# A hybrid attention and convolution block: the first two value blocks in one group, three of six pair sums brought by transfer, and another deal of the layer-norm steps

## The chip, the cores and the metric

The kernel runs on one core of a Trainium2 chip. A core has a matrix engine (PE in the profile; PEld is its weight load), a vector engine (DVE), an activation engine (ACT), GpSimd (POOL) and a queue engine (SP) that issues most transfers. Each engine executes its own list of instructions strictly in order and waits on semaphores for the others. The metric is the device time of one execution, in microseconds (us).

## What is computed

One layer on a sequence of 256 positions with 4096 channels. After an RMS norm, one large product gives seven column groups, and two branches use them. Cut to what matters here:

```python
xn = rms_norm(x, norm_in_g)
q, k, v, z_a, a_c, g_c, z_c = split(xn @ w_in)      # each 2048 columns wide
y_a = rms_norm(chunked_attention(q, k, v, table)) * silu(z_a)      # 16 heads of 128
u   = a_c * sigmoid(g_c)                            # GLU
u   = silu(layer_norm(causal_depthwise_conv(u, 31 taps)))
y_c = rms_norm(u @ w_pw + b_pw) * silu(z_c)
h   = x + concat(y_a, y_c) @ w_out
h  += sigmoid(rms_norm(h) @ w_ple_gate + b) * (p @ w_ple)
out = rms_norm(h)
```

All is in float32. For the matrix engine each float32 operand is split into a high and a low part, and a product is three matmuls: high by high, low by high, high by low.

## The kernel before

**Tiles.** The 256 positions are two halves `h` of 128. A block is 512 output columns (`NB`). The 4096 input channels are 32 blocks of 128, or 16 pairs. One matmul multiplies 128 channels of one half with 512 columns.

**A single block** (`product`, line 235) takes 32 channel blocks x 2 halves x 3 = 192 matmuls. ACT makes the high part of each weight tile and DVE the low part (`parts_of`, lines 199 to 210: `wh` and `wl`, three buffers each).

**Two blocks as one group** (`mixed_product`, line 339) run over the 16 channel pairs. A plain pair costs 2 x 2 x 2 x 3 = 24 matmuls. A pair marked `*` or `+` is done by a Strassen-Winograd step: seven products in place of eight, 21 matmuls, at the price of sums of weight tiles. With `*` the DVE makes four sums for a pair (lines 464, 465, 471, 472: two into `ua`, two into `ub`). With `+` the first two sums come by transfer: SP loads one part into `ua` and GpSimd adds the other with an accumulating transfer (lines 417 and 418), and the DVE makes only the other two, in place. The orders in which the pairs are taken are the strings in lines 329 to 337; `early` has four `+` steps, `early_six` six `*` steps. From the first to the last such step the group holds all four temporary PSUM banks for its helper sums (`P1`, `P5`, `P7`, `P6`); the same four banks serve transposes and attention at other times. At the end ACT and DVE combine the helpers (`helper_sums`, line 505) and fold the accumulators into the result (line 533).

**Work dealt out in between.** Convolution taps and layer-norm steps are small DVE and ACT jobs in a queue (`later`). After each pair of a group, `fill(n)` takes n jobs from it (line 182); the numbers per pair are `early_fills`, `six_fills`, or `(4,)`.

**Order of the stages.** `glu_conv(c)` makes one input group (the columns `a_c` and `g_c` of block c as one pair), the GLU, and puts 124 taps in the queue. `heads(g)` makes q and k of four heads as one group, transposes them (`to_heads`), makes v as a single block and runs `attention`. The list before is: input groups 0 and 1, heads 0, input group 2, heads 1, input group 3, heads 2, the layer norm's jobs into the queue, heads 3. Then follow the pointwise product, the z groups, `w_out` and the gate. I call the groups glu0 to glu3, qk0 to qk3, v0 to v3, and the attention of four heads attn0 to attn3.

The text gives a program order. A planner in the framework moves instructions between each other's waiting times by its own estimates, so the order on each engine is written into the program when it is built, and does not adapt when it runs.

Of the kernel before, what the change touches and what calls it, by code (L numbers as in the profile page):

```python
# [25 lines left out]
def hybrid_block(  # L26
# [137 lines left out]
    def transposed(src, blocks, then=lambda ins: None):  # L164

        pt = tmp_psum()
        for i, b in enumerate(blocks):
            for h in range(NH):
                last_transpose[:] = [
                    nc.tensor.transpose(  # L170
                        pt[:, i * T + h * P : i * T + (h + 1) * P],
                        src[:, h, b * P : (b + 1) * P],
                        ident,
                    )
                ]
                then(*last_transpose)
        return [pt[:, i * T : (i + 1) * T] for i in range(len(blocks))]
# [151 lines left out]
    dense = units("1 0* 3 2* 5 4* 6* 7 8* 9 10* 11 12* 14* 13 15")  # L329
    first = units("0 1 3 5 7 9 11 13 15 2* 8 4* 10 6* 12 14")  # L330
    early = units("1 3 5 0+ 7 9 2+ 11 13 4+ 15 8 6+ 10 12 14")
    early_six = units("1 3 5 7 0* 9 2* 11 4* 13 6* 15 8* 10* 12 14")

    early_fills = (5, 6, 1, 5, 6, 1, 5, 6, 1, 5, 6, 1, 2, 5, 5, 4)
    six_fills = (4, 6, 7, 1, 5, 1, 5, 1, 5, 1, 2, 4, 6, 6, 6, 4)
    final = units("1 0* 3 2* 5 4* 6* 7 8* 9 10* 12* 11 13 14 15")
    late = units("1 3 5 7 9 11 13 15 0* 2 4* 6 8* 10* 12 14")

    def mixed_product(
# [86 lines left out]
        for n, (pair, seven) in enumerate(order):  # L426
            if n < done:
                continue
            if ahead:
                ahead(pair)  # L430
            wts = []
            for k in range(2):
                wt = wpool.tile([P, 2, NB], F32, tag="w", name="wt")
                if seven == "+" and k == 0:
                    nc.sync.dma_start(wt[:, 0], w[2 * pair * P : (2 * pair + 1) * P, col : col + NB])
                else:
                    nc.sync.dma_start(wt, two_columns(w, 2 * pair + k, col, apart))
                wts.append(wt)
            sums_ahead(n)
            if n >= len(order) - n_left:  # L440
                for k in range(2):
                    tiles = left[2 * (n - len(order) + n_left) + k]
                    held.append((2 * pair + k, parts_of(wts[k], 2, tiles and tiles())[0]))
                fill(fills[n % len(fills)])
                continue
            if not seven:
                for k in range(2):
                    add_plain(n, k, *parts_of(wts[k], 2)[0])
                fill(fills[n % len(fills)])
                continue  # L450
            begins = not helper
            if begins:
                for name in ("P1", "P5", "P7", "P6"):
                    helper[name] = ps_tmp.tile([P, NB], F32, tag="tmp", name=f"acc_{name}")
                banks.update(helper)
            w0, w1 = wts
            plus = partial(nc.vector.tensor_tensor, op=ALU.add)
            before = list(recent)
            w0h, w0l = parts_of(w0, 1)[0]
            if seven == "+":  # L460
                ua = ub = sums[n]
            else:
                ua = upool.tile([P, 2, NB], F32, tag="u", name="ua")
                plus(ua[:, 0], w0[:, 0], w0[:, 1])  # L464
                plus(ua[:, 1], w0[:, 1], w1[:, 1])  # L465
            with queued_behind(before if seven == "+" else ()):
                uah, ual = pair_parts(ua)
            w1h, w1l = parts_of(w1, 2)[0]
            if seven != "+":
                ub = upool.tile([P, 2, NB], F32, tag="u", name="ub")  # L470
            plus(ub[:, 0], ua[:, 0], w1[:, 1])
            plus(ub[:, 1], ub[:, 0], w1[:, 0])  # L472
# [12 lines left out]
            add("P3", s_of(3), (w1h[:, 1], w1l[:, 1]), n, True)  # L485
            add("P6", s_of(2), (ubh[:, 0], ubl[:, 0]), n, True)
            add("P4", block(k1, 1), (ubh[:, 1], ubl[:, 1]), n, True)
            if begins and on_begin:
                on_begin()
            if begins:  # L490
                tc.add_manual_dep(
                    made[first].ins, last_transpose[0].ins.name,
                    mybir.DependencyInfo(mybir.DependencyClass.NoSync, mybir.DependencyReason.DATA),
                    reason="transposes before the helpers take their banks",
                )
            if n == last_seven:
                on_helpers(helper)
            fill(fills[n % len(fills)])
# [12 lines left out]
        tt(z[1][0], helper["P7"], z[1][0], ALU.add)  # L511
        tt(z[1][1], helper["P5"], z[1][0], ALU.add)

    def sum_tiles():

        t = [spool.tile([P, NH, NB], F32, tag="stage", name="z") for _ in range(2)]
        return t, [[t[j][:, h] for j in range(2)] for h in range(NH)]

    def scaled_pair(w, col, apart, order, r, fills, **kw):

        t, z = [], []

        def on_helpers(helper):
            for dst, src in zip((t, z), sum_tiles()):
# [13 lines left out]

    def square_sum(dst, src, scale=1.0):
        junk = spool.tile([P, NB], mybir.dt.bfloat16, tag="junk", name="junk", bufs=1)  # L540
        return nc.scalar.activation(junk[:, : src.shape[1]], src, AF.Square, scale=scale, accum_out=dst)

    def rstd_of(partial, n, name):
        r = cpool.tile([P, partial.shape[1]], F32, name=name)
# [222 lines left out]
    def layer_norm_swish():  # L767
# [1 line left out]
        add = nc.vector.tensor_tensor  # L769
        st = {}  # L770

        def hd_tile(name):
            return spool.tile([P, 4, T], F32, tag="hd", name=name, bufs=5)
# [90 lines left out]
    y_a = []  # L864
    ssq_a = cpool.tile([P, NH, AW // NB], F32, name="ssq_a")

    def to_heads(st, name):

        t = spool.tile([P, GH, T], F32, tag="hd", name=name, bufs=5)
        for pair in range(GH // 2):  # L870
            pt = tmp_psum()
            for i in range(2):
# [9 lines left out]
            )  # L882
        return t

    def attention(g, qT, kT, v, bias):
        y = act.tile([P, NH, NB], F32, tag="act", name="y_a")
        for hd in range(GH):
            sp = tmp_psum()
            nc.tensor.matmul(sp[:, :P], qT[:, hd, :P], kT[:, hd, :P], start=True, stop=True)
# [25 lines left out]
            nc.tensor.matmul(o[:, HD : 2 * HD], pT[:, 2 * P :], v[:, 1, vc], start=False, stop=True)  # L915
            for h in range(NH):
                nc.scalar.activation(
                    y[:, h, vc], o[:, h * HD : (h + 1) * HD], AF.Identity, scale=den[:, h : h + 1]
                )
        for h in range(NH):  # L920
            square_sum(ssq_a[:, h, g : g + 1], y[:, h, :])
        y_a.append(y)

    def heads(g):
        nonlocal more
        bias = spool.tile([P, GH, T], F32, tag="hd", name="bias", bufs=5)
        span = 2 * MAXR + 1
        nc.sync.dma_start(
            bias,
# [9 lines left out]
        if g == n_g - 1:  # L939
            first_sums.close()  # L940
            more = pool("more", 4)
        accv = product(w_in0, o_v + g * NB, xT, KD)
        v = spool.tile([P, NH, NB], F32, tag="hd", name="v", bufs=5)
        for h in range(NH):
            nc.scalar.activation(v[:, h, :], accv[h], AF.Identity, scale=r_x[:, h : h + 1])
        attention(g, qT, kT, v, bias)

    n_g = H // GH
    assert n_g == CW // NB
# [68 lines left out]
    def gated(ys, c0, col, r_y, order, ahead):  # L1018
# [6 lines left out]

        acc = mixed_product(w_in0, col + c0 * NB, xT, xS, order, on_helpers, ahead=ahead, fills=(2,))
        for h, j in QUARTERS:
            zz, y = z[h][j], ys[c0 + j][:, h, :]
            tt(zz, acc[h][j], zz, ALU.subtract if j else ALU.add)  # L1029
            nc.scalar.activation(zz, zz, AF.Silu, scale=r_x[:, h : h + 1])  # L1030
            later.append(partial(stt, y, y, r_y[:, h : h + 1], zz, ALU.mult, ALU.mult))

    def before_last(make):
# [278 lines left out]
```

## Time and profile before

| | |
|---|---|
| median of 3 runs | 2039.11 us (2038.57 to 2039.72) |
| the profiled execution | 2040.98 us |
| its span, first to last instruction | 2039.2 us |
| PE busy | 2019.7 us, 99% |
| DVE busy | 1860.4 us, 91% |
| ACT busy | 1198.3 us, 59% |
| granted PE clock, mean | 0.997 |

The profile's views used here are these. The page gives busy time per engine. The table by stretches gives, for each stretch of time, the stretch's length and then the busy time and the number of instructions (x) of each engine, the granted clock, the share of the DMA engines that was busy and GB/s. The groups give for one line, operation and tile the count, the busy time, the mean duration in ns of one, and the idle time of the engine ahead of them with what ended it. The chain is the path of work that ended last, followed back from the end: start, length, what. The timeline gives single instructions in order of time, with the idle time before them in square brackets.

By the chain and the tiles' names the stages of the profiled execution lie so: glu0 to 102 us, glu1 to 187, qk0 to 270, v0 to 315, attn0 and glu2 to 408, qk1 to 495, v1 to 539, attn1 and glu3 to 633, qk2 to 716, v2 to 760, attn2 and qk3 to 860, v3 to 904.

### The profile page before, as it was taken

The page shows a single profiled execution, that of the slowest core. Times are in us where ns is not written, and L with a number is a line of the kernel's source. Part 1 is how long each engine was busy: PE and PEld are TensorE (multiplying, and loading weights), DVE is VectorE, ACT ScalarE, POOL GpSimd, SP SyncE. Part 2 cuts the span into 40 slices and gives each one's busy share as a digit, 9 for nine tenths or more (in the row PEclk, how much of TensorE's full clock was granted, in tenths as well). Part 3 has the DMA queues.
Part 4 walks back from the last instruction along what each step waited for, and adds up shares of the span by engine and source line. Part 5 has one row for each costly group of instructions (what it writes and reads, how often), then busy time and mean ns, then how long its engine had stood idle before and what let it go on. Part 6 is the DMA issues. An engine that isn't in the chain of part 4 may idle for free.

```text
span 2039.2 us, 26104 instructions
## 1 busy us (share of the span) xinstructions
PE 2019.7 (99%) x9106; PEld 1662.4 (82%) x9106; DVE 1860.4 (91%) x2640; ACT 1198.3 (59%) x1559; POOL 37.5 (2%) x43
## 2 busy tenths in 40 slices
PE   9999999999999999999999999999999999999997
PEld 7888888888888888788888888888888888888876
DVE  7999998699889977868899999999999999999998
ACT  7655446454555545666556566676565666655555
POOL 0000000000000000000000000000000000000000
PEclk9999999999999999999999999999999999999999
DMA  8787866876568866565666666676666656666765
GB/s 292 222 238 234 256 199 180 253 227 187 175 189 265 254 188 204 160 186 203 195 211 201 196 211 200 220 236 204 213 201 205 214 185 207 200 220 204 234 209 177
DMA packets 171839, 431.18 MB, mean 211 GB/s; under 512 B 13742, under 2 KB 16958, under 8 KB 171706
## 3 DMA queue, kind: packets, MB, share of 16 engines
q1 hardware_dynamic: 164528, 416.09, 63.2%
q0 software_dynamic: 6528, 12.58, 3.8%
q8 instruction: 71, 1.16, 0.2%
q10 hardware_dynamic: 650, 0.84, 0.1%
q14 instruction: 62, 0.51, 0.1%
HBM read 425.26 MB, written 4.19 MB: 211 GB/s over the span
## 4 chain that ended last, share of the span: by engine, by line
PE 91%; DVE 6%; issue 2%; DMA 0%; ACT 0%; POOLq 0%; POOL 0%; ACTq 0%; DVEq 0%
PE acc L382 65%; PE acc_P L382 16%; PE acc L229 7%; DVE wl L205 2%; DVE cv L718 2%; PE tmp_ps L170 1%; DMA wt<-in_w_in_dram 0%; PE tmp_ps L890 0%; PE tmp_ps L908 0%; PE tmp_ps L875 0%; PE tmp_ps L913 0%; PE acc L370 0%; PE tmp_ps L125 0%; DVE ul L205 0%; PE tmp_ps L915 0%
## 5 line engine op out<-in xcount | busy, mean ns | idle before, releaser
L382 PE MATMUL acc<-wh,big_t 128*128 128x512 f32 x3788 | 1172.0, 392 | 1.8 <-DVE z L1029 1.1
L204 ACT CAST wh<-wt 128x1024 fp32r<-128x1024 f32 (+1 forms) x737 | 715.7, 980 | 579.0 <-PE acc L382 353.6
L205 DVE TENSOR_TENSOR wl<-wt,wh 128x1024 fp32r<-128x1024 f32 (+1 forms) x737 | 824.5, 1131 | 91.3 <-ACT wh L204 86.0
L382 PEld LDWEIGHTS acc<-wh,big_t 128*128 128x128 f32 x3788 | 708.9, 188 | 149.1 <-ACT wh L204 1.5
L382 PE MATMUL acc<-wl,big_t 128*128 128x512 f32 x1894 | 732.3, 392 | 2.8 <-DVE wl L205 2.8
L382 PEld LDWEIGHTS acc<-wl,big_t 128*128 128x128 f32 x1894 | 355.8, 188 | 77.7 <-DVE wl L205 4.2
L718 DVE SCALAR_TENSOR_TENSOR cv<-uT,dw,cv 128x250 f32<-128x250 f32 (+21 forms) x480 | 200.5, 462 | 1.2
L204 ACT CAST uh<-ua 128x1024 fp32r<-128x1024 f32 x146 | 153.6, 1052 | 67.1 <-DVE ua L465 46.4
L205 DVE TENSOR_TENSOR ul<-ua,uh 128x1024 fp32r<-128x1024 f32 x146 | 177.9, 1218 | 7.6 <-ACT uh L204 7.4
L229 PE MATMUL acc<-wh,big_t 128*128 128x512 f32 x560 | 173.6, 390 | 0.0
L204 ACT CAST uh<-ub 128x1024 fp32r<-128x1024 f32 x98 | 103.1, 1052 | 98.5 <-DVE ub L472 70.6
L382 PE MATMUL acc_P<-uh,big_t 128*128 128x512 f32 x504 | 154.2, 391 | 0.1
L205 DVE TENSOR_TENSOR ul<-ub,uh 128x1024 fp32r<-128x1024 f32 x98 | 119.6, 1221 | 6.7 <-ACT uh L204 6.1
L229 PEld LDWEIGHTS acc<-wh,big_t 128*128 128x128 f32 x560 | 105.1, 188 | 21.6
L382 PEld LDWEIGHTS acc_P<-uh,big_t 128*128 128x128 f32 x504 | 93.5, 188 | 21.9 <-ACT uh L204 3.1
L229 PE MATMUL acc<-wl,big_t 128*128 128x512 f32 x280 | 108.9, 389 | 0.0
L382 PE MATMUL acc_P<-ul,big_t 128*128 128x512 f32 x252 | 96.5, 391 | 0.0
L464 DVE TENSOR_TENSOR ua<-wt 128x512 f32<-128x512 f32 x98 | 67.3, 687 | 22.6 <-DMA wt<-in_w_in_dram 17.0
L382 PE MATMUL acc<-uh,big_t 128*128 128x512 f32 x244 | 75.6, 390 | 0.0
L382 PE MATMUL acc_P<-wh,big_t 128*128 128x512 f32 x244 | 75.3, 389 | 0.0
L465 DVE TENSOR_TENSOR ua<-wt 128x512 f32<-128x512 f32 x98 | 67.1, 685 | 3.2 <-DMA wt<-in_w_in_dram 2.1
L472 DVE TENSOR_TENSOR ub<-ub,wt 128x512 f32<-128x512 f32 x98 | 67.3, 687 | 1.0
(244 smaller groups left out, 1575.6 us busy)
## 6 DMA issues: line engine op xcount, KB each, us to landing
wt<-in_w_in_dram SPq DMA_DIRECT2D x423, 512.0 KB, 4.4
wt<-in_w_out_dram SPq DMA_DIRECT2D x128, 512.0 KB, 4.3
wt<-in_w_ple_gate_dram SPq DMA_DIRECT2D x128, 512.0 KB, 4.1
wt<-in_w_pw_dram SPq DMA_DIRECT2D x32, 512.0 KB, 4.5
ua<-in_w_in_dram SPq DMA_DIRECT2D x24, 512.0 KB, 4.3
ua<-in_w_in_dram POOLq DMA_DIRECT2D x24, 512.0 KB, 8.2
wt<-in_w_in_dram SPq DMA_DIRECT2D x24, 256.0 KB, 2.7
hc<-in_x_dram SPq DMA_DIRECT2D x8, 512.0 KB, 5.3
```

Source lines behind the costliest of these rows:

```text
L170: nc.tensor.transpose(pt[:, i * T + h * P : i * T + (h + 1) * P], src[:, h, b * P : (b + 1) * P], ident,)
L204: nc.scalar.copy(wh[:, :kc, :], wt[:, :kc, :]),
L205: nc.vector.tensor_tensor(wl[:, :kc, :], wt[:, :kc, :], wh[:, :kc, :].bitcast(F32), ALU.subtract),
L229: nc.tensor.matmul(acc, a, b[:, k, :], start=kb == 0 and kind == 0, stop=kb == kblocks - 1 and kind == 2,)
L382: nc.tensor.matmul(banks[name], a, b, start=name not in begun, stop=final and ends[name] == n and kind == 2 and not (left and name in "P2 ...
L464: plus(ua[:, 0], w0[:, 0], w0[:, 1])
L465: plus(ua[:, 1], w0[:, 1], w1[:, 1])
L472: plus(ub[:, 1], ub[:, 0], w1[:, 0])
L718: nc.vector.scalar_tensor_tensor(cv[:, i, PAD - k :], uT[:, i, : T + k - PAD], dw[:, b, k : k + 1], cv[:, i, PAD - k :], ALU.mult, ALU.add,)
```

## The change

Three things are changed together, with some moving of buffers that makes room for them.

1. v0 and v1 are made as one group of two blocks (`paired_values(0, early, early_fills, ...)`) after qk0, with four `+` steps, and v1's single product is gone. Attention of heads 1 then follows directly on qk1. The heads' q tile moves to the pool `act`, and attention writes its result in place over it, seen through another view; the two value tiles take buffers of the pool `hd`.
2. The order of glu3, `early_six`, has three of its six steps as `+` in place of `*`, starts them at the fourth pair instead of the fifth, and its `*` steps make their second sums in place (one buffer fewer). `six_fills` is dealt anew.
3. qk3 gets `norm_fills` in place of `(4,)`: two jobs after three of the four `+` steps, five after most plain pairs; the sum stays 64.

```diff
-    early_six = units("1 3 5 7 0* 9 2* 11 4* 13 6* 15 8* 10* 12 14")
+    early_six = units("1 3 5 0+ 7 2* 9 4+ 11 6* 13 8+ 15 10* 12 14")
 
     early_fills = (5, 6, 1, 5, 6, 1, 5, 6, 1, 5, 6, 1, 2, 5, 5, 4)
-    six_fills = (4, 6, 7, 1, 5, 1, 5, 1, 5, 1, 2, 4, 6, 6, 6, 4)
+    six_fills = (6, 6, 1, 5, 1, 5, 1, 5, 1, 5, 1, 5, 1, 6, 7, 7)
+    norm_fills = (5, 5, 2, 5, 5, 2, 5, 5, 2, 5, 5, 2, 2, 4, 5, 5)
...
-                ua = upool.tile([P, 2, NB], F32, tag="u", name="ua")
+                ua = ub = upool.tile([P, 2, NB], F32, tag="u", name="ua")
                 plus(ua[:, 0], w0[:, 0], w0[:, 1])
                 plus(ua[:, 1], w0[:, 1], w1[:, 1])
...
-            if seven != "+":
+            if seven == "*" and not sums:
                 ub = upool.tile([P, 2, NB], F32, tag="u", name="ub")
...
-    def scaled_pair(w, col, apart, order, r, fills, **kw):
+    def scaled_pair(w, col, apart, order, r, fills, home={}, **kw):
...
-    def attention(g, qT, kT, v, bias):
-        y = act.tile([P, NH, NB], F32, tag="act", name="y_a")
+    def attention(g):
+        qT, kT, v, bias = qs[g], ks.pop(g), vs.pop(g), biases.pop(g)
+        y = qT.rearrange("q g (h d) -> q h g d", h=NH)
...
-        q, k = scaled_pair(w_in0, o_q + g * NB, o_k - o_q, early, r_x, (4,) if g == n_g - 1 else early_fills)
-        qT, kT = to_heads(q, "qT"), to_heads(k, "kT")
...
+    def keys(g, fills):
+        q, k = scaled_pair(w_in0, o_q + g * NB, o_k - o_q, early, r_x, fills)
+        qs[g] = act.tile([P, GH, T], F32, tag="act", name="qT")
+        to_heads(q, qs[g])
+        ks[g] = hd_tile("kT")
+        to_heads(k, ks[g])
+
+    def paired_values(g, order, fills, **kw):
+        vs[g], vs[g + 1] = scaled_pair(w_in0, o_v + g * NB, NB, order, r_x, fills, **kw)
...
     glu_conv(0)
-    for g in range(n_g):
-        if g + 1 < n_g:
-            glu_conv(g + 1)
-        else:
-            layer_norm_swish()
-        heads(g)
+    glu_conv(1)
+    load_bias(0)
+    keys(0, early_fills)
+    paired_values(0, early, early_fills, home=dict(tag="hd", bufs=5))
+    attention(0)
+    glu_conv(2)
+    load_bias(1)
+    keys(1, early_fills)
+    attention(1)
+    glu_conv(3)
+    load_bias(2)
+    keys(2, early_fills)
+    single_values(2)
+    attention(2)
+    layer_norm_swish()
+    load_bias(3)
+    keys(3, norm_fills)
+    first_sums.close()
+    more = pool("more", 4)
+    single_values(3)
+    attention(3)
```

The places that later read the attention's result (`square_sum`, `gated`, `transposed`) take the other view of the tile; their instruction counts stay.

More of the change, by code (lines that the diff above doesn't have):

```diff
@@ L171, in transposed @@
                         pt[:, i * T + h * P : i * T + (h + 1) * P],
-                        src[:, h, b * P : (b + 1) * P],
+                        src[:, h, b] if len(src.shape) == 4 else src[:, h, b * P : (b + 1) * P],
                         ident,
@@ L512, in helper_sums, with sum_tiles @@
         tt(z[1][1], helper["P5"], z[1][0], ALU.add)
-    def sum_tiles():
-        t = [spool.tile([P, NH, NB], F32, tag="stage", name="z") for _ in range(2)]
+    def sum_tiles(**kw):
+        kw = kw or dict(tag="stage")
+        t = [spool.tile([P, NH, NB], F32, name="z", **kw) for _ in range(2)]
         return t, [[t[j][:, h] for j in range(2)] for h in range(NH)]
-    def scaled_pair(w, col, apart, order, r, fills, **kw):
+    def scaled_pair(w, col, apart, order, r, fills, home={}, **kw):
         t, z = [], []
         def on_helpers(helper):
-            for dst, src in zip((t, z), sum_tiles()):
+            for dst, src in zip((t, z), sum_tiles(**home)):
                 dst.extend(src)
@@ L540, in square_sum @@
         junk = spool.tile([P, NB], mybir.dt.bfloat16, tag="junk", name="junk", bufs=1)
-        return nc.scalar.activation(junk[:, : src.shape[1]], src, AF.Square, scale=scale, accum_out=dst)
+        to = junk.rearrange("q (g d) -> q g d", d=src.shape[2]) if len(src.shape) == 3 else junk[:, : src.shape[1]]
+        return nc.scalar.activation(to, src, AF.Square, scale=scale, accum_out=dst)
     def rstd_of(partial, n, name):
@@ L770, in layer_norm_swish @@
         st = {}
-        def hd_tile(name):
-            return spool.tile([P, 4, T], F32, tag="hd", name=name, bufs=5)
         def fold(s):
@@ L865, in hybrid_block, with to_heads @@
     ssq_a = cpool.tile([P, NH, AW // NB], F32, name="ssq_a")
-    def to_heads(st, name):
-        t = spool.tile([P, GH, T], F32, tag="hd", name=name, bufs=5)
+    def to_heads(st, t):
         for pair in range(GH // 2):
@@ L917, in attention, with hd_tile, load_bias @@
                 nc.scalar.activation(
-                    y[:, h, vc], o[:, h * HD : (h + 1) * HD], AF.Identity, scale=den[:, h : h + 1]
+                    y[:, h, hd], o[:, h * HD : (h + 1) * HD], AF.Identity, scale=den[:, h : h + 1]
                 )
         for h in range(NH):
-            square_sum(ssq_a[:, h, g : g + 1], y[:, h, :])
+            square_sum(ssq_a[:, h, g : g + 1], y[:, h])
         y_a.append(y)
-    def heads(g):
-        nonlocal more
-        bias = spool.tile([P, GH, T], F32, tag="hd", name="bias", bufs=5)
+    qs, ks, vs, biases = {}, {}, {}, {}
+    def hd_tile(name):
+        return spool.tile([P, GH, T], F32, tag="hd", name=name, bufs=5)
+    def load_bias(g):
+        bias = biases[g] = hd_tile("bias")
         span = 2 * MAXR + 1
@@ L936, in heads, with single_values @@
         nc.gpsimd.memset(bias[: P // 2, :, : P // 2], NEG)
-        q, k = scaled_pair(w_in0, o_q + g * NB, o_k - o_q, early, r_x, (4,) if g == n_g - 1 else early_fills)
-        qT, kT = to_heads(q, "qT"), to_heads(k, "kT")
-        if g == n_g - 1:
-            first_sums.close()
-            more = pool("more", 4)
+    def keys(g, fills):
[6 more added lines that the diff above has]
+        vs[g], vs[g + 1] = scaled_pair(w_in0, o_v + g * NB, NB, order, r_x, fills, **kw)
+    def single_values(g):
         accv = product(w_in0, o_v + g * NB, xT, KD)
-        v = spool.tile([P, NH, NB], F32, tag="hd", name="v", bufs=5)
+        vs[g] = spool.tile([P, NH, NB], F32, tag="hd", name="v", bufs=5)
         for h in range(NH):
-            nc.scalar.activation(v[:, h, :], accv[h], AF.Identity, scale=r_x[:, h : h + 1])
-        attention(g, qT, kT, v, bias)
+            nc.scalar.activation(vs[g][:, h, :], accv[h], AF.Identity, scale=r_x[:, h : h + 1])
     n_g = H // GH
-    assert n_g == CW // NB
+    assert n_g == CW // NB == 4
     glu_conv(0)
-    for g in range(n_g):
-        if g + 1 < n_g:
-            glu_conv(g + 1)
-        else:
-            layer_norm_swish()
-        heads(g)
+    glu_conv(1)
[19 more added lines that the diff above has]
+    attention(3)
     r_a = rstd_of(ssq_a, AW, "r_a")
@@ L1027, in gated @@
         for h, j in QUARTERS:
-            zz, y = z[h][j], ys[c0 + j][:, h, :]
+            zz, y = z[h][j], ys[c0 + j][:, h]
             tt(zz, acc[h][j], zz, ALU.subtract if j else ALU.add)
             nc.scalar.activation(zz, zz, AF.Silu, scale=r_x[:, h : h + 1])
+            if len(y.shape) == 3:
+                zz = zz.rearrange("q (g d) -> q g d", d=HD)
             later.append(partial(stt, y, y, r_y[:, h : h + 1], zz, ALU.mult, ALU.mult))
```

## The prediction

> **What bounds the kernel now.** I read the page first: busy times and the chain that ended last.
>
> ```profile
> span 2039.2 us, 26104 instructions
> ...
> PE 2019.7 (99%) x9106; PEld 1662.4 (82%) x9106; DVE 1860.4 (91%) x2640; ACT 1198.3 (59%) x1559; POOL 37.5 (2%) x43
> ...
> PE 91%; DVE 6%; issue 2%; DMA 0%; ACT 0%; POOLq 0%; POOL 0%; ACTq 0%; DVEq 0%
> ```
>
> PE is nearly always busy and is 91% of the chain, so a matmul less is time saved, as long as nothing makes PE wait. Whether busy also means at full pace is seen in two long unbroken pieces of the chain, start, length, what:
>
> ```profile
> 428.94 11.56 PE acc L382 x51
> 495.01 43.34 PE acc L229 x191
> ```
>
> 11.56 / 51 and 43.34 / 191 both give 0.227 us for a 512-column matmul, in a group and in a single block alike. That is PE's pace and the price of one matmul. The table by stretches tells where the DVE, at 91%, has room:
>
> ```profile
> core 0: us, PE busy (x) PEld busy (x) DVE busy (x) ACT busy (x) POOL busy (x), PEclk, DMA share, GB/s
> 187.00:270.00 83.00, 83.00 (x372) 68.76 (x371) 83.00 (x138) 42.14 (x46) 5.17 (x5) 1.00 0.84 246
> 270.00:315.00 45.00, 45.00 (x208) 37.44 (x207) 45.00 (x86) 18.84 (x20) 0.00 (x0) 1.00 0.61 182
> 315.00:408.00 93.00, 92.85 (x430) 76.53 (x429) 66.78 (x94) 54.27 (x81) 4.87 (x4) 1.00 0.75 219
> 408.00:495.00 87.00, 87.00 (x397) 72.09 (x396) 86.95 (x142) 47.22 (x54) 2.74 (x3) 1.00 0.70 212
> 495.00:539.00 44.00, 44.00 (x197) 36.47 (x196) 38.59 (x69) 17.92 (x19) 0.00 (x0) 1.00 0.65 192
> 539.00:633.00 94.00, 94.00 (x436) 77.22 (x434) 76.75 (x101) 61.55 (x90) 2.44 (x2) 1.00 0.67 202
> 760.00:860.00 100.00, 97.16 (x451) 79.53 (x450) 75.56 (x107) 59.76 (x90) 3.46 (x4) 0.98 0.61 182
> ```
>
> The rows are qk0, v0, attn0 with glu2, qk1, v1, attn1 with glu3, and attn2 with qk3. In qk0 and v0 the DVE is busy throughout and PE still loses nothing: convolution taps that nobody waits for fill its spare time. Only the last row shows PE losing, 2.84 us, and a mean clock under 1. PE's waits and its timeline there:
>
> ```profile
> PE acc L382 <- DVE wl L205: 2.8, 1, 2.8
> ```
>
> ```profile
> 841.24 1.97 PE L382 MATMUL acc<-wh,big_t 128*128 128x512 f32 x8
> 846.05 2.08 PE L382 MATMUL acc<-wl,big_t 128*128 128x512 f32 x4 [2.84 <-DVE wl L205]
> 847.92 1.05 PE L382 MATMUL acc<-wh,big_t 128*128 128x512 f32 x2
> ...
> 849.80 0.40 PE L382 MATMUL acc<-wl,big_t 128*128 128x512 f32 x1
> ```
>
> Eight matmuls from 841.24 at 0.227 would let the next start at 843.05; it starts at 846.05: 3.00 us lost. The 9 matmuls from 846.05 to 849.80 take 3.75 us where 9 x 0.227 is 2.04: another 1.71 at the lower clock. 4.7 us in all, the one sizeable hole in the part that the change touches. The DVE's timeline shows what it did meanwhile:
>
> ```profile
> 833.43 1.23 DVE L205 TENSOR_TENSOR wl<-wt,wh 128x1024 fp32r<-128x1024 f32 x1 [0.78 <-ACT wh L204]
> 834.58 3.10 DVE L799 TENSOR_TENSOR cv<-cv,mu 128x256 f32<-128x256 f32 x9
> 837.60 0.68 DVE L509 TENSOR_TENSOR z<-acc_P,z 128x512 f32<-128x512 f32 x1
> 838.20 0.42 DVE L799 TENSOR_TENSOR cv<-cv,mu 128x256 f32<-128x256 f32 x1
> 838.53 1.23 DVE L807 TENSOR_TENSOR sq<-sq 128x1024 f32<-128x1024 f32 x1
> 839.68 0.68 DVE L510 TENSOR_TENSOR z<-acc_P,z 128x512 f32<-128x512 f32 x1
> ...
> 844.77 2.36 DVE L205 TENSOR_TENSOR wl<-wt,wh 128x1024 fp32r<-128x1024 f32 x2
> ```
>
> From 834.58 to 844.77, 10.19 us, no low part of a weight is made: 16 layer-norm subtractions, four helper sums and two additions of squares stand between.
>
> **The change, part by part.** Durations are from the profiled execution, 2040.98 us with a span of 2039.2; the median is 1.87 below it. I subtract from the profiled execution and carry the difference to the median.
>
> ```profile
> L205 DVE TENSOR_TENSOR wl<-wt,wh 128x1024 fp32r<-128x1024 f32 x615 | 743.7, 1219 | 87.3 <-ACT wh L204 83.9 <-PE tmp_ps L170 1.5 <-DMA dw_rows<-in_w_dw_dram 0.5
> L205 DVE TENSOR_TENSOR ul<-ua,uh 128x1024 fp32r<-128x1024 f32 x146 | 177.9, 1218 | 7.6 <-ACT uh L204 7.4
> L205 DVE TENSOR_TENSOR wl<-wt,wh 128x512 fp32r<-128x512 f32 x122 | 83.5, 685 | 4.0 <-ACT wh L204 2.0 <-PE acc L382 2.0
> L464 DVE TENSOR_TENSOR ua<-wt 128x512 f32<-128x512 f32 x98 | 67.3, 687 | 22.6 <-DMA wt<-in_w_in_dram 17.0 <-DMA wt<-in_w_out_dram 4.1 <-DMA wt<-in_w_ple_gate_dram 1.1
> L472 DVE TENSOR_TENSOR ua<-ua,wt 128x512 f32<-128x512 f32 x24 | 16.4, 685 | 0.2
> L533 DVE SCALAR_TENSOR_TENSOR z<-acc,r_x,z 128x512 f32<-128x512 f32 x32 | 22.0, 746 | 3.9 <-PE acc L382 3.9
> L509 DVE TENSOR_TENSOR z<-acc_P,z 128x512 f32<-128x512 f32 x20 | 13.8, 688 | 2.1 <-PE acc_P L382 1.6 <-issue 0.2
> ```
>
> *v0 and v1 as a group, PE.* Two single blocks are 2 x 192 = 384 matmuls; a group with four steps is 16 x 24 - 4 x 3 = 372. Twelve fewer: 12 x 0.227 = 2.72 us, all on the path.
>
> *The same, DVE.* A `+` step makes a half low part (0.685), a full one (1.219), two in-place sums (2 x 0.685) and two low parts of sums (2 x 1.218): 5.7 us, against 2 x 1.219 = 2.4 for a plain pair; four steps add 13.1. At the end come four helper sums (4 x 0.688) and four folds (4 x 0.746) where ACT alone had evacuated v: 5.7 more. In all 18.8 us of DVE. What covers it: the group needs 12 x 2.4 + 4 x 5.7 + 5.7, about 58 us, of 372 x 0.227 = 84.4, so the rest is left for taps; those that no longer fit go to the stage after attn0, where the row 315:408 leaves the DVE idle for 26.2 of 93 us. qk0 has just this shape and pace of DVE work, and its row shows no PE loss. In the built order of the changed kernel the DVE's work ahead of each weight part, measured against PE's matmuls, keeps the same distance through the new group as through qk0. I cost this at 0; if the cover fails, the price is the overrun, up to a few us (rivals). ACT gains about as many casts as it loses evacuations and is half idle in all these rows.
>
> *The same, transfers.* Each `+` step moves 256 + 512 + 512 KB by SP and 512 KB by GpSimd in place of 1024 KB. With glu3 there are seven: seven more transfers in SP's queue and seven more accumulating ones in POOL's, and 5.4 MB. The new group's DMA share should rise from v0's 0.61 to qk0's 0.84, where PE lost nothing. Cost 0. The bias load of heads 1 now waits for attn0's reads as it did before.
>
> *attn1 directly behind qk1.* What is queued behind the removed v1: the q and k transposes, the copies and attn1's first scores now follow each other with two matmuls between. The rows at the end of qk1:
>
> ```profile
> 491.37 2.71 DVE L533 SCALAR_TENSOR_TENSOR z<-acc,r_x,z 128x512 f32<-128x512 f32 x4
> ...
> 494.00 2.34 DVE L205 TENSOR_TENSOR wl<-wt,wh 128x1024 fp32r<-128x1024 f32 x2
> ...
> 494.72 1.08 ACT L880 COPY kT<-tmp_ps 128x512 f32<-128x512 f32 x2
> 494.76 0.48 PE L229 MATMUL acc<-wh,big_t 128*128 128x512 f32 x1
> ```
>
> The first k copy ends at 494.72 + 0.54 = 495.3, and two matmuls from 494.76 end their turn at about the same time: 0.1 us. After that the scores' DVE work of each head stands behind taps, sums for glu3 and weight parts, some 3.5 to 5.6 us per head in the built order, against roughly 4 to 5 us of PE work that the planner put between. A head can lose 0.2 to 0.3 us. I take 0.6 for attn1; ends 0 and 4 x 1.3 (a weight part, 1.219, late in every head).
>
> *glu3.* Matmuls stay (16 x 24 - 6 x 3). The DVE loses six sums, 6 x 0.687 = 4.1 us; its row has 17 us idle, so that buys nothing. The in-place sums of the `*` steps wait for both parts of the first sums; taps stand in the gap. 0, ends 0 and 3 x 0.7.
>
> *qk3's deal.* In the built order 13 subtractions, four helper sums and one addition stand between the same two low parts, not 16, 4 and 2. Steps by the starts above: 0.335 (3.02 / 9), 0.60, 1.15: 13 x 0.335 + 4 x 0.60 + 1.15 = 7.9 us in place of 10.2. The weight part then ends at 834.58 + 7.9 + 1.2 = 843.7 where PE needs it at 843.05: 0.7 lost, not 3.0. What is late next: the sum of squares comes after qk3's last matmul instead of before it, so two folds of qk3 stand on the DVE behind it and behind the wait for the variance; v3's accumulators need them. I count 0.7 at v3's first matmul and 0.35 at the other half. So 1.75 lost where 4.7 were, a gain of about 3.0. The ends are no gain and 4.7.
>
> Whether so short a wait lowers the clock is shown by another one:
>
> ```profile
> 1243.74 0.70 PE L382 MATMUL acc<-wh,big_t 128*128 128x512 f32 x2 [1.14 <-DVE z L1029]
> 1244.28 0.40 PE L382 MATMUL acc<-wl,big_t 128*128 128x512 f32 x1
> ```
>
> 1.14 us idle, and the matmuls behind go on at full pace; only the 2.84 us wait was followed by slow ones. So the 1.71 go with the long wait. [...]
>
> *Sum:* -2.72 - 3.0 + 0.6 = -5.1 us. 2040.98 - 5.1 = 2035.9 for a profiled execution, 2039.11 - 5.1 = 2034.0 for the median.
>
> **The rivals.**
>
> *The layer norm's wait only moves.* qk3's end is a chain DVE, PE, DVE, GpSimd, DVE (variance, inverse root, spread), now interleaved with v3's first matmuls. If 3.4 of the 4.7 us are lost again there, 1.3 is won, and with 2.0 lost in attn1, inside its ends, the sum is -2.72 - 1.3 + 2.0 = -2.0: 2037.1. For it: the variance is moved behind the last matmul. Against: the whole stretch from mean to variance is longer by 18 matmuls, 4.1 us.
>
> *The slow clock was in the profiled execution only.* The profiled run is 1.87 us above the median, about the 1.71 of the slow clock. Then the median gains that much less: 2034.0 + 1.7 = 2035.7. [...] Against: the three runs lie within 1.15 us.
>
> *The hole closes entirely* and attn1 costs nothing: -2.72 - 4.7 = -7.4, 2031.7. Against: 7.9 us between two low parts is still longer than three buffers of 12 matmuls hold for certain.
>
> *Slower: attn1 waits for the DVE in every head.* The row of qk1 shows the DVE busy for 86.95 of 87 us, so it enters attn1 with no reserve, and v1's 44 us that gave it room are gone. If each of four heads waits for two weight parts (2 x 1.219) the loss is 9.8 against a gain of 5.7: +4.1, and with one long wait that slows the clock +5: 2044. It decides from 5.7 / 4 = 1.4 us per head. Against: PE lost nothing at qk0 into v0 with the DVE as full.
>
> **How the numbers follow.** Under 0.2% (4.08 us) a measurement of this kernel can hardly be told from no change; faster means below 2035.0, slower above 2043.2. Forecast 0.48 (2032.6 to 2035.8, four fifths of it below 2035.0); moved wait 0.17 (same); clock only in the profile 0.12 (mostly same); closed hole 0.12 (faster); slower 0.11. Faster 0.38 + 0.12 + 0.04 = 0.54, same 0.35, slower 0.11. The range goes from the closed hole, 2031.5, to the middle between the moved wait and the slower case, 2040.0; it leaves out most of the slower case and some of both tails.
>
> **What will show it.** The values pair: 372 matmuls at 0.227 without gaps. qk3: PE's longest wait for a weight part below 1 us and the clock at 1.00. attn1: PE's loss between its scores and transposes below 1 us. Wrong would be waits of over 1 us on the DVE in attn1 or in the new group, or a new wait at v3's start above 1.5 us.

## The result and the profile after

The changed kernel takes 2032.67 us (median of 6 runs, 2032.07 to 2034.37), the kernel before in the same session 2039.26: a ratio of 0.9969 with a 95% interval of 0.9958 to 0.9979, 4.3 to 8.6 us less. 2034.0 was predicted, so it is faster, by 1.3 us more than forecast; the interval is wider than that difference. The profiled execution took 2032.83 us, its span is 2031.1 us, 8.1 us shorter than that of before.

The page of the changed kernel, busy times and the chain:

```profile
span 2031.1 us, 26144 instructions
...
PE 2015.5 (99%) x9094; PEld 1658.7 (82%) x9094; DVE 1871.1 (92%) x2658; ACT 1203.3 (59%) x1568; POOL 46.0 (2%) x50
...
PE 92%; DVE 5%; issue 2%; ACT 1%; DMA 1%; POOLq 0%; POOL 0%; ACTq 0%; DVEq 0%
```

Twelve matmuls fewer (9106 to 9094), 10.7 us more of the DVE, seven more POOL operations. The table by stretches of the changed kernel, with the rows of the values group, of attn0 with glu2, qk1, attn1 with glu3, and attn2 with qk3:

```profile
core 0: us, PE busy (x) PEld busy (x) DVE busy (x) ACT busy (x) POOL busy (x), PEclk, DMA share, GB/s
...
270.00:354.00 84.00, 84.00 (x380) 69.72 (x379) 83.68 (x138) 43.56 (x49) 4.87 (x4) 1.00 0.80 232
354.00:448.00 94.00, 94.00 (x435) 77.33 (x434) 62.66 (x80) 53.09 (x80) 4.87 (x4) 1.00 0.74 218
448.00:534.00 86.00, 85.98 (x386) 70.92 (x385) 85.95 (x142) 45.97 (x51) 5.18 (x5) 1.00 0.81 239
534.00:628.00 94.00, 94.00 (x441) 77.44 (x440) 90.46 (x147) 59.62 (x90) 3.65 (x3) 1.00 0.70 205
...
757.00:854.00 97.00, 96.47 (x448) 78.64 (x448) 73.52 (x105) 58.29 (x86) 3.46 (x4) 1.00 0.64 189
```

PE is busy for all of the new group (84.00 of 84) and of attn1 with glu3, though the DVE is nearly full in both. The last row has lost 0.53 us in place of 2.84, and its clock is 1.00. PE's timeline there, and the DVE's:

```profile
838.51 1.98 PE L383 MATMUL acc<-wh,big_t 128*128 128x512 f32 x8
841.01 1.20 PE L383 MATMUL acc<-wl,big_t 128*128 128x512 f32 x4 [0.53 <-DVE wl L205]
842.05 0.62 PE L383 MATMUL acc<-wh,big_t 128*128 128x512 f32 x2
```

```profile
831.86 2.77 DVE L799 TENSOR_TENSOR cv<-cv,mu 128x256 f32<-128x256 f32 x8
...
838.74 1.08 DVE L799 TENSOR_TENSOR cv<-cv,mu 128x256 f32<-128x256 f32 x3
839.75 2.35 DVE L205 TENSOR_TENSOR wl<-wt,wh 128x1024 fp32r<-128x1024 f32 x2
```

The stretch in which the DVE makes no low part of a weight is 839.75 - 831.86 = 7.89 us (10.19 before). By starts, the eight matmuls from 838.51 would let the next begin at 840.32; it begins at 841.01, 0.69 late (3.00 before), and the matmuls behind it keep the pace of 0.227.

I add up what PE loses against 0.227 us from each start to the next. Of the 8.1 us, 2.72 are the twelve matmuls; 4.0 are qk3's hole (4.71 to 0.69, and nothing at v3's start); about 0.4 is lost anew at the end of qk1 and in attn1. Another 1.1 to 1.3 us (idle, or from start to start) is the wait at 1243 us of the kernel before, in the z group, which the changed trace does not have; the rest is many waits below 0.4 us.

### The profile page after: what moved, and what is told of

The parts are those of the page before. It is cut to its first block, busy times and chain, and to the rows that moved or that the text cites. A ratio compares the mean times of both kernels' runs of the same rounds, so it can differ in the third digit from the quotient of the medians.

```text
span 2031.1 us, 26144 instructions
## 1 busy us (share of the span) xinstructions
PE 2015.5 (99%) x9094; PEld 1658.7 (82%) x9094; DVE 1871.1 (92%) x2658; ACT 1203.3 (59%) x1568; POOL 46.0 (2%) x50
## 3 DMA queue, kind: packets, MB, share of 16 engines
q8 instruction: 71, 1.16, 0.2%
## 4 chain that ended last, share of the span: by engine, by line
PE 92%; DVE 5%; issue 2%; ACT 1%; DMA 1%; POOLq 0%; POOL 0%; ACTq 0%; DVEq 0%
PE acc L383 67%; PE acc_P L383 16%; PE acc L229 5%; DVE wl L205 2%; PE tmp_ps L170 1%; DVE cv L721 1%; DMA wt<-in_w_out_dram 0%; PE tmp_ps L890 0%; DVE ul L205 0%; PE tmp_ps L874 0%; PE tmp_ps L908 0%; PE tmp_ps L913 0%; ACT wh L204 0%; PE acc L371 0%; DVE cv L799 0%
## 5 line engine op out<-in xcount | busy, mean ns | idle before, releaser
L383 PE MATMUL acc<-wh,big_t 128*128 128x512 f32 x3992 | 1234.7, 391 | 0.7 <-DVE y_c L1030 0.3
L383 PEld LDWEIGHTS acc<-wh,big_t 128*128 128x128 f32 x3992 | 746.8, 188 | 155.1 <-issue 0.9
L383 PE MATMUL acc<-wl,big_t 128*128 128x512 f32 x1996 | 770.7, 391 | 0.6 <-DVE wl L205 0.5
L383 PEld LDWEIGHTS acc<-wl,big_t 128*128 128x128 f32 x1996 | 374.3, 188 | 79.5 <-DVE wl L205 2.3
L204 ACT CAST uh<-ua 128x1024 fp32r<-128x1024 f32 x160 | 168.3, 1052 | 80.9 <-DVE ua L466 46.1
L721 DVE SCALAR_TENSOR_TENSOR cv<-uT,dw,cv 128x250 f32<-128x250 f32 (+19 forms) x480 | 202.3, 463 | 1.1
L205 DVE TENSOR_TENSOR ul<-ua,uh 128x1024 fp32r<-128x1024 f32 x160 | 194.9, 1218 | 8.4 <-ACT uh L204 8.0
L204 ACT CAST uh<-ub 128x1024 fp32r<-128x1024 f32 x92 | 96.8, 1053 | 95.8 <-DVE ub L473 86.5
L205 DVE TENSOR_TENSOR ul<-ub,uh 128x1024 fp32r<-128x1024 f32 x92 | 112.2, 1220 | 6.1 <-ACT uh L204 5.2
L229 PE MATMUL acc<-wh,big_t 128*128 128x512 f32 x304 | 93.9, 390 | 0.0
L229 PEld LDWEIGHTS acc<-wh,big_t 128*128 128x128 f32 x304 | 56.9, 188 | 11.9 <-issue 0.2
L383 PE MATMUL acc_P<-uh,comb_t 128*128 128x512 f32 x216 | 66.4, 390 | 0.1
```

The source lines that it names most:

```text
L204: nc.scalar.copy(wh[:, :kc, :], wt[:, :kc, :]),
L205: nc.vector.tensor_tensor(wl[:, :kc, :], wt[:, :kc, :], wh[:, :kc, :].bitcast(F32), ALU.subtract),
L229: nc.tensor.matmul(acc, a, b[:, k, :], start=kb == 0 and kind == 0, stop=kb == kblocks - 1 and kind == 2,)
L383: nc.tensor.matmul(banks[name], a, b, start=name not in begun, stop=final and ends[name] == n and kind == 2 and not (left and name in "P2 ...
L721: nc.vector.scalar_tensor_tensor(cv[:, i, PAD - k :], uT[:, i, : T + k - PAD], dw[:, b, k : k + 1], cv[:, i, PAD - k :], ALU.mult, ALU.add,)
```

## The experiments

All times stand beside runs of the kernel before on the same chip, whose median moved between 2039.1 and 2039.7 from session to session; "less" is against that. The interval of a ratio is about 0.001 to each side, 2 us, so differences between variants of 1 us are read from the traces and only supported by the times.

**One part alone, and one part undone.** The deal alone, on the kernel before:

```diff
-        q, k = scaled_pair(w_in0, ..., early, r_x, (4,) if g == n_g - 1 else early_fills)
+        q, k = scaled_pair(w_in0, ..., early, r_x, norm_fills if g == n_g - 1 else early_fills)
```

> The kernel before with the dealt layer norm steps in qk3 and nothing else. Theory (the prediction's term, put right by the trace of the changed kernel): the hole of 4.9 us at 842 shrinks to about 1.0 and nothing comes back at v3's start, so a gain of 3.9 us, 2035.3 against 2039.2, and the wait of 1.1 us at 1242 in the gated stage stays (2034.2 if it goes too). The prediction as put on record: 3.0 gained, 2036.2. Rival (the slow clock was in the profiled execution only): 2.2 gained or less, 2037 or more.

By their places in the list the numbers of `norm_fills` give two jobs after the plain pair directly ahead of each `+` step and after the last `+` step, and five after the first three `+` steps, not two after three of the steps as the list of changes says.

Measured: 2037.14 us, 2.6 less, ratio 0.9987 (0.9978 to 0.9996). 3.9 less was expected, so by the time alone the rival (2037 or more) would stand as well; what decides is how often the slow clock comes, below.

```profile
841.90 1.98 PE L382 MATMUL acc<-wh,big_t 128*128 128x512 f32 x8
844.76 1.21 PE L382 MATMUL acc<-wl,big_t 128*128 128x512 f32 x4 [0.88 <-DVE wl L205]
845.80 1.78 PE L382 MATMUL acc<-wh,big_t 128*128 128x512 f32 x7
```

The wait there is 1.04 us from start to start (0.88 idle), with no slow matmuls behind. In the trace the hole is 3.6 us shorter; 0.3 of that is lost to a longer wait in the z group, which this trace has too, at 1240.8 us.

The changed kernel with the old deal:

```diff
-    keys(3, norm_fills)
+    keys(3, (4,))
```

> The changed kernel with the old deal of four steps per group of weights in qk3. Theory: the hole comes back with its full length, 4.9 us in place of 1.0, so 2032.7 + 3.9 = 2036.6; PE's clock is lowered again behind a wait of about 2.8 us. Rival (slow clock in the profiled execution of before only): the wait of 3 us is there at full clock behind it, 2034.9. Open: whether the wait of 1.1 us at 1242 comes back with it (then 2037.7).

Measured: 2034.67 us, 5.1 less, ratio 0.9973 (0.9962 to 0.9984). The hole did not come back in full: PE waits 1.36 us there, not 3.00, with the old deal. So the deal was not the only part that shortens it.

The values group alone (the old deal, and glu3's old order and fills):

```diff
-    early_six = units("1 3 5 0+ 7 2* 9 4+ 11 6* 13 8+ 15 10* 12 14")
-    six_fills = (6, 6, 1, 5, 1, 5, 1, 5, 1, 5, 1, 5, 1, 6, 7, 7)
+    early_six = units("1 3 5 7 0* 9 2* 11 4* 13 6* 15 8* 10* 12 14")
+    six_fills = (4, 6, 7, 1, 5, 1, 5, 1, 5, 1, 2, 4, 6, 6, 6, 4)
-    keys(3, norm_fills)
+    keys(3, (4,))
```

> The changed kernel with the old deal in qk3 and the old steps of the fourth input group: the values group alone is left. Theory: 12 matmuls fewer, 2.72 us less, and nothing lost in attn1: 2039.2 - 2.7 = 2036.5. By the prediction's term for attn1 (0.6 lost): 2037.1. Rival (the scores wait for the DVE in each head): 2043.

Measured: 2037.09 us, 2.65 less, ratio 0.9983 (0.9974 to 0.9992). The group is worth its matmuls. The hole is there in full (3.00 us and slow matmuls), no head of attn1 has a wait worth naming: PE is busy for 93.79 of the 94 us of attn1 with glu3.

Glu3's old steps in the changed kernel (the first four changed lines above, with the new deal kept):

> The changed kernel with the old six steps in the fourth input group, all six computing their sums on the DVE. Theory: the DVE has 4.1 us more to do in a stage with 3.5 us idle and taps to put off, so no difference from the changed kernel, 2032.7, within 0.5. Rival: the sums by transfer are what keeps the stage free of waits, and with v1's 44 us gone the old steps cost 1 us or more, 2033.7 or more, with PE waits for the DVE in 534 to 628.

Measured: 2034.16 us, 5.6 less, ratio 0.9974 (0.9964 to 0.9984), about 1 us slower than the changed kernel, inside the interval. The time lies in the rival's range, but the place does not bear the rival out: the trace shows no new wait for the DVE in glu3 (PE loses 2.1 us in attn1 with glu3, 1.9 in the changed kernel). The wait in qk3 is 1.03 in place of 0.69.

So glu3's new lines shorten a wait two stages later. Set side by side, the new `six_fills` hand out 63 jobs and the old 64. Without the values group the jobs run out by the end of glu3; with it they run out in glu2 already, and by glu3's end 64 + 64 jobs are asked for against 128 taps and combinations there: 63 leaves one over, so that each layer-norm step comes one place later.

**One job more.** The old deal, and only the last number of glu3's deal changed:

```diff
-    six_fills = (6, 6, 1, 5, 1, 5, 1, 5, 1, 5, 1, 5, 1, 6, 7, 7)
+    six_fills = (6, 6, 1, 5, 1, 5, 1, 5, 1, 5, 1, 5, 1, 6, 7, 8)
```

> The changed kernel with the old deal in qk3, and the fourth input group's last step given 8 things to run in place of 7, so that its steps hand out 64 as before the change and not 63. Theory (the new steps of the fourth input group help only by handing out one thing less, which moves every layer norm step one place back in qk3 and so one addition out of the long stretch): the stretch is 10.2 us again, PE waits about 3.0 us and runs slow behind it, and the time goes from 2034.7 to that of the values group alone, 2037.1. Rival (the sums by transfer are worth it themselves): the wait stays near 1.4 us and the time at 2034.7.

Measured: 2037.24 us, 1.9 less, ratio 0.9989 (0.9980 to 0.9998): 2.6 slower than with 63, by one job (3.2 when each is set against the kernel before of its own session). This kernel has the sums by transfer and lands where the values group alone does (2037.09), so these sums by themselves bring nothing. The DVE's timeline, first with 63 jobs (the old deal), then with 64:

```profile
832.00 2.77 DVE L799 TENSOR_TENSOR cv<-cv,mu 128x256 f32<-128x256 f32 x8
...
838.88 1.76 DVE L799 TENSOR_TENSOR cv<-cv,mu 128x256 f32<-128x256 f32 x5
840.55 1.22 DVE L205 TENSOR_TENSOR wl<-wt,wh 128x1024 fp32r<-128x1024 f32 x1
841.94 1.23 DVE L807 TENSOR_TENSOR sq<-sq 128x1024 f32<-128x1024 f32 x1 [0.16 <-ACT sq L803]
```

```profile
831.99 3.10 DVE L799 TENSOR_TENSOR cv<-cv,mu 128x256 f32<-128x256 f32 x9
...
839.55 1.08 DVE L799 TENSOR_TENSOR cv<-cv,mu 128x256 f32<-128x256 f32 x3
840.70 1.22 DVE L807 TENSOR_TENSOR sq<-sq 128x1024 f32<-128x1024 f32 x1
841.84 0.42 DVE L799 TENSOR_TENSOR cv<-cv,mu 128x256 f32<-128x256 f32 x1
842.18 2.35 DVE L205 TENSOR_TENSOR wl<-wt,wh 128x1024 fp32r<-128x1024 f32 x2
```

With 63 the second addition of squares (1.15 us) stands behind the low part, with 64 ahead of it: the stretch is 8.55 or 10.19 us, PE's wait 1.36 or 2.99.

The same idea on the kernel before, one job fewer in glu3:

```diff
-    six_fills = (4, 6, 7, 1, 5, 1, 5, 1, 5, 1, 2, 4, 6, 6, 6, 4)
+    six_fills = (4, 6, 7, 1, 5, 1, 5, 1, 5, 1, 2, 4, 6, 6, 6, 3)
```

> The kernel before with one number changed: the fourth input group hands out 63 things, not 64. Theory: the wait at 842 falls from 3.0 to about 1.4 us and the slow matmuls behind it go, 3.4 us less, 2039.5 to about 2036.5 (2037 by what the new steps gave in the changed kernel). Rival (the sums by transfer): no change, 2039.5.

Measured: 2039.95 us, ratio 1.0002 (0.9993 to 1.0011), no change; the stretch is 10.22 us and the wait 3.00. The expectation was wrong: in the kernel before, the queue of jobs is empty at the end of glu3, with eight places in the deal to spare, so one place less moves nothing. Fifteen fewer move it by seven:

```diff
-    six_fills = (4, 6, 7, 1, 5, 1, 5, 1, 5, 1, 2, 4, 6, 6, 6, 4)
+    six_fills = (4, 6, 7, 1, 5, 1, 5, 1, 5, 1, 2, 3, 3, 3, 2, 0)
```

> The kernel before with the last six numbers of the fourth input group's deal changed, 49 things handed out in place of 64. In the kernel before the queue runs dry there, so the first eight fewer change nothing (which is why one fewer changed nothing); seven are left over and move the layer norm seven places back in qk3. In the built order 10 subtractions and four helper sums then stand between the low parts, 10 x 0.335 + 4 x 0.60 = 5.8 us in place of 10.2. Theory (the layer norm's wait is only a matter of where its steps fall): PE does not wait at 842 at all and runs at full clock, 4.5 us less in the mean, 2034.7. Rival (the deal by units, or the sums by transfer, is needed): a wait of over 1 us stays, 2037 or more.

Measured: 2035.46 us, 4.1 less, ratio 0.9978 (0.9969 to 0.9988). Its DVE timeline:

```profile
834.69 1.43 DVE L799 TENSOR_TENSOR cv<-cv,mu 128x256 f32<-128x256 f32 x4
836.03 0.69 DVE L509 TENSOR_TENSOR z<-acc_P,z 128x512 f32<-128x512 f32 x1
...
839.43 1.09 DVE L799 TENSOR_TENSOR cv<-cv,mu 128x256 f32<-128x256 f32 x3
840.44 2.35 DVE L205 TENSOR_TENSOR wl<-wt,wh 128x1024 fp32r<-128x1024 f32 x2
```

The stretch is 5.75 us and PE does not wait. Five numbers in a deal two stages earlier close the hole that the new deal in qk3 alone only shortens. Over the traces the wait is the stretch less 7.2 us:

| kernel | stretch without a low part, us | PE's wait, start to start, us |
|---|---|---|
| before, values alone, 64 jobs | 10.2 | 3.0 |
| changed, old deal | 8.55 | 1.36 |
| new deal alone; changed, old glu3 | 8.23 | 1.04 |
| changed | 7.89 | 0.69 |
| before with 49 jobs; changed with 59 | 5.75 | 0 |

**The same for the changed kernel, and six steps in more groups.**

```diff
-    six_fills = (6, 6, 1, 5, 1, 5, 1, 5, 1, 5, 1, 5, 1, 6, 7, 7)
+    six_fills = (6, 6, 1, 5, 1, 5, 1, 5, 1, 5, 1, 4, 1, 5, 6, 6)
```

> The changed kernel with 59 things handed out in the fourth input group in place of 63: 10 subtractions and four helper sums between the low parts. Theory: the last 0.69 us of wait at 840 go, 2032.5 to 2031.8. Rival: the steps moved back make v3's folds late and PE waits there for 0.7 or more, 2032.5 or more.

Measured: 2032.19 us, 7.4 less, ratio 0.9963 (0.9950 to 0.9975). The wait at 840 is gone and v3's start has none; between this and the changed kernel (0.9969) the times do not decide.

```diff
-                ahead=more_combinations if last else None,
+                ahead=more_combinations if c == 2 else None,      # and early_six for glu2 as for glu3
-    keys(1, early_fills)
+    keys(1, (5, 5, 0, 4, 0, 3, 0, 4, 0, 3, 0, 3, 0, 3, 3, 3), early_six)
-    single_values(2)
+    single_values(2, 3)
```

> The kernel of the run with 59, with the combinations for pairs 8 and 10 made in glu2 and kept, and six steps of 21 matmuls in glu2 and qk1 as well: 12 matmuls fewer, 12 x 0.227 = 2.7 us. Taps are dealt so that qk1 has 36 and v2 48. Theory (the DVE idles 31 us in attn0 with glu2, so this is covered as the values group was): 2031.8 - 2.7 = 2029.1. Rival (qk1, where the DVE is busy for 85.95 of 86 us, can't take two more such steps): PE waits for the DVE in 448 to 534 and half of it or more is lost, 2030.5 or more.

Measured: 2032.22 us, ratio 0.9961 (0.9949 to 0.9974), no gain over the run before it, though 12 matmuls are gone (9082); 2029.1 was expected. The deals of glu2 and glu3 were changed with it. The stretches of attn0 with glu2, qk1, and attn1 with glu3:

```profile
354.00:448.00 94.00, 94.00 (x433) 76.84 (x432) 76.96 (x106) 56.21 (x83) 3.65 (x3) 1.00 0.70 211
448.00:534.00 86.00, 85.99 (x386) 70.52 (x385) 85.54 (x128) 49.59 (x56) 3.96 (x4) 1.00 0.77 233
534.00:628.00 94.00, 94.00 (x439) 77.67 (x438) 92.98 (x154) 59.13 (x89) 3.65 (x3) 1.00 0.69 205
```

The rival had the time right, but qk1 has no wait of any length, so its place is not where the gain went. Against the trace of the run before, PE loses 1.0 us more in pieces of 0.1 to 0.2 us in glu2 and qk1, 0.9 more at the start of the kernel, ahead of everything that was edited, and 1.6 in pieces elsewhere. Whether the rest belongs to the kernel or to the execution five runs do not tell.

**The clock behind the wait, and the wait at 1243 us.** The kernel before once more, unchanged:

> The kernel before, unchanged. Theory (the slow clock behind a 3 us wait is decided anew in each execution): the wait at 842 is 3.00 us again, within 0.05, and the nine matmuls behind it take anything from 2.04 to 3.75 us; the runs spread over some 3 us where those of the changed kernel spread over 2. Rival (the clock falls behind every such wait): 3.75 us again. The wait of 1.14 us at 1242: again 1 us or more if the order of this kernel makes it, gone or smaller if it hangs on when a fetch of instructions falls into a weight transfer.

Measured: 2039.62 us, ratio 0.9999 (0.9990 to 1.0009). The timeline of this execution, then that of the kernel with one job fewer, at the same place:

```profile
841.16 1.97 PE L382 MATMUL acc<-wh,big_t 128*128 128x512 f32 x8
845.97 1.91 PE L382 MATMUL acc<-wl,big_t 128*128 128x512 f32 x4 [2.83 <-DVE wl L205]
847.68 1.06 PE L382 MATMUL acc<-wh,big_t 128*128 128x512 f32 x2
848.53 0.63 PE L382 MATMUL acc<-wl,big_t 128*128 128x512 f32 x1
848.96 0.93 PE L382 MATMUL acc<-wh,big_t 128*128 128x512 f32 x2
849.73 0.39 PE L382 MATMUL acc<-wl,big_t 128*128 128x512 f32 x1
```

```profile
840.88 1.97 PE L382 MATMUL acc<-wh,big_t 128*128 128x512 f32 x8
845.69 1.20 PE L382 MATMUL acc<-wl,big_t 128*128 128x512 f32 x4 [2.83 <-DVE wl L205]
846.72 0.62 PE L382 MATMUL acc<-wh,big_t 128*128 128x512 f32 x2
```

The same wait, 2.83 us idle; in the first, matmuls start 0.43 us apart until 849 and 1.71 us is lost, in the second they run on at 0.227. Of the six profiles with this wait (the kernel before twice, one job fewer, the values group alone, 64 jobs, and the kernel with 112 more instructions below), one lost 0.1 us behind it, four 1.7 and one 2.9; of the five profiles with a wait of 0.69 to 1.36 us there, none lost more than 0.2. The longest wait in between, 1.94 us idle at 602 in the kernel with 112 more instructions, has no slow matmuls behind it either.

The wait at 1243 did not recur in this execution of the same program. The transfer of weights that caused it took 5.75 us in the first profile,

```profile
1232.93 5.75 DMA wt<-in_w_in_dram
```

and 4.53 us in this one. It had come in one more profile, that of the deal alone, where the same transfer was later still:

```profile
1229.65 6.08 DMA wt<-in_w_in_dram
```

The cause that the next two expectations name is a fetch of 16 KB of instructions (the page of the kernel before has 71 packets, 1.16 MB, in this instruction queue), which by the trace of the kernel before started 3.6 us after the transfer was issued. Two kernels, run ahead of this one, were to move the fetch by more instructions on PE, cutting idle warming matmuls into pieces:

```diff
-            pin(nc.tensor.matmul(idle_ps, idle[:, :P], idle, start=True, stop=True))
+            for lo in range(0, 512, 64):      # the other kernel: (0, 256), (256, 384), (384, 512)
+                pin(nc.tensor.matmul(idle_ps[:, lo:lo + 64], idle[:, :P], idle[:, lo:lo + 64], start=True, stop=True))
```

> The kernel before with the first eight warming matmuls cut into eight each, 112 instructions more on PE: the fetches come some 12.7 us earlier, that of 1236.56 at about 1223.9. Theory: the transfer issued at 1232.9 takes 4.2 to 4.5 us in place of 5.75, and PE's wait of 1.14 us at 1242 is gone or below 0.4. [...] Rival: the wait stays at 1.1 us.

> The changed kernel with the first five warming matmuls cut into three each, 20 instructions more on PE and as many columns: every later fetch of PE's instructions comes some 2.3 us earlier against the matmuls. Theory (the wait at 1242 of the kernel before is a weight transfer held up by such a fetch of 16 KB): the fetch at 1230.9 moves to about 1228.6, into the transfer that now takes 4.36 us; that takes 5.5 us or more, and PE waits 1 us or so at about 1234 where it waits for nothing. The time is 1 us longer. Rival (the wait comes from how the attention outputs are stored): no wait there, 2032.7.

Measured: the kernel before so changed has no wait there, a transfer of 4.37 us, and new waits elsewhere (2.1 us from start to start at 600); 2041.84 us, ratio 1.0013 (1.0004 to 1.0022). 40 of the cut matmuls took the 2.31 us that the five whole ones had taken. The changed kernel so changed: 2032.47 us, ratio 0.9965 (0.9953 to 0.9977), and no wait; but against the transfers its fetch came only 0.8 us earlier, not 2.3, and met no more than the last 0.5 us of the transfer. So these two settle nothing.

The other profiles do. In five of them such a fetch starts 3.1 to 3.6 us after this transfer is issued. In two it is late (5.75 us in the kernel before, 6.08 with the deal alone); in three it is not (4.53 in the second execution of the kernel before, 4.18 with one job fewer, 4.36 with 49 jobs). So the fetch alone is not the cause. The same program has the wait in one execution and not in another, and what makes it stays open.

## Why the prediction was right, and where its steps were off

- *v0 and v1 as a group, 2.72 us on the path, DVE and transfers at 0.* Right: twelve matmuls fewer, no gap in the group, DMA share 0.80 (0.84 was said). That the time came out 2.65 less, so near, is luck: the interval of that run is 1.6 to 5.3 us. The DVE's busy time rose by 14.0 us there (1860.4 to 1874.4), less than the 18.8 of durations added up.
- *attn1 behind qk1, 0.6.* Right in size: about 0.4, in pieces; the slower rival (9.8 us in four heads) is out, with the DVE 85.95 of 86 us busy just ahead.
- *glu3 at 0.* This step failed, in its reason: the sums by transfer cost and gain nothing in glu3, but the new deal hands out one job less than are there, and that alone is worth about 2.5 us in qk3 (2037.1 or 2037.2 to 2034.7; 2.4 to 3.2 when each is set against its own session's kernel before). The text costed the step by its own stage and did not ask what a shorter deal hands on.
- *qk3's deal, 3.0 gained.* The size of the whole hole was right: the built order gave 7.9 us for the stretch and 0.7 for the wait, 7.89 and 0.69 were measured. But that order held both edits, and the text booked all of it under the deal. So the sum came out although its parts were booked wrongly. The deal brings 2.6 us alone. On top of the others the medians differ by 2.0, but PE's wait only by 0.67 (1.36 to 0.69); the rest of the two traces' difference comes in pieces of 0.5 us or less outside qk3, and no run ties it to the deal. Of 1.75 us that were to be lost, the 1.05 at v3's start was not, which is the term that was mis-sized. PE's timeline of the changed kernel at that place, without a wait:

```profile
850.21 0.67 PE L229 MATMUL acc<-wh,big_t 128*128 128x512 f32 x2
850.72 0.50 PE L814 MATMUL tmp_ps<-mean_w,sq 128*128 128x1 f32 x4
...
853.02 0.61 PE L827 MATMUL tmp_ps<-lnsum,mean_w 128*128 128x128 f32 x4
853.47 1.91 PE L874 MATMUL tmp_ps<-ident,z 128*128 128x128 f32 x16
```

  v3's matmuls, the two statistics and the 16 transposes of q and k fill the time in which the DVE folds. By the trace this is most of the 1.3 us between 2034.0 and 2032.7; the times alone do not resolve so little.
- *The slow clock goes with the long wait.* Right: five of the six long waits (2.8 us idle) have it, none of the five short ones (0.5 to 1.2 us idle) has. In the first profile of the kernel before the granted clock is 0.57 in the mean from 846 to 850 us, and 1.00 from 838 to 846 and from 850 to 856. The rival that it was in the profiled execution only is out: the second profile of the same program has it too, as have those of the values group alone and of 64 jobs. Behind the same 2.83 us idle the kernel with one job fewer ran on at 0.227 us a matmul; no run shows what decides it.
- *The hole closes entirely* was a rival with 2031.7; it did not close, but the kernels with 49 and 59 jobs show it can.
- *Not foreseen:* the wait at 1243 us of the kernel before does not come in every execution: it is in the first profile and in that of the deal alone, and not in the second profile of the same program. It makes the two spans differ by 1.1 to 1.3 us more than the kernels do.

## What to carry to other kernels

When jobs are dealt from a queue by fixed numbers, a number changed in one stage moves every later job; count what is left in the queue at each stage's end, and look for the cost where the moved jobs land. Here PE's wait was the stretch of DVE work ahead of the awaited weight part less 7.2 us in every trace with a wait there (from 7.89 and 0.69 us to 10.2 and 3.0); the built order, with the durations measured before the change, had given 7.9 and 0.7 for the changed kernel, so both could be read before it ran. Undo parts one at a time before crediting any of them, and profile the unchanged kernel twice before a single wait of 1 us is booked.

## What was not expected of the hardware

A wait of 3.0 us cost 4.7 us in four of six profiles, since PE ran at about half pace (0.43 us from start to start) for 3.0 to 3.4 us behind it or soon after; it cost 5.9 in one and 3.1 in one. Waits in the same place of up to 1.36 us cost at most 0.2 us more than themselves. A transfer of 512 KB in the same place of the same program took 4.53 us in one execution and 5.75 in another. Five warming matmuls cut into eight pieces each took 2.31 us, as they had whole. A fetch of instructions did not come earlier by as much as was worked out from the instructions added ahead of it: 20 more instructions on PE moved it by 0.8 us against the transfers, not 2.3.
